# A four-row SwiGLU stream: the middle stores move from the Activation queue to the SP queue, ahead of the next loads

## The chip, the cores and the metric

The kernel runs on one core of one Trainium2 chip; the other cores of the chip run nothing of it. The metric is the device time of one execution in microseconds. Three runs of the kernel before took 964.71, 965.05 and 966.81 us, a median of 965.05 us. Beside them one execution was profiled; it took 966.08 us, of which the trace spans 964.3 us.

## The reference

```python
def setup_inputs():
    return {"x": np.random.randn(8192, 8192).astype(np.float32)}

def reference(x):
    a, b = np.split(x, 2, axis=-1)
    silu_b = b / (1 + np.exp(-b))
    return a * silu_b
```

Each of the 8192 rows holds 4096 values of `a`, then 4096 values of `b`. The output is 8192 x 4096 in float32. So 268.44 MB are read and 134.22 MB are written, 402.66 MB in all, and each element of the output needs one Silu and one product.

## The kernel before

**Tiling.** A partition takes four consecutive rows, so a group is 128 partitions x 4 rows = 512 rows, and 8192 rows make G = 16 groups (`last` is 15). The input of a group comes as two loads of 128 x 16384 float32 (8.39 MB, 64 KB in each partition): the *first* load brings rows 0 and 1 of each partition into one of two buffers, `packs[g % 2]`, and the *second* brings rows 2 and 3 into the single buffer `extra`. The output of a group, again 128 x 16384, is one store. So there are 48 transfers of equal size: 16 first loads, 16 extra loads, 16 stores.

**Compute of a group** (the function `swiglu`, lines 63 and 65). ScalarE applies Silu to `b` in place, and VectorE multiplies by `a`. It is done three times for a group: once for the two rows in the pack (128x8192), and once for each of the two rows in `extra` (128x4096). The products all go into the same pack: those of the first two rows to its first half, where the rows just read lay, and those of `extra` to its second half. The last product of a group is called `prod` in the code.

**Buffers.** `extra` is free for the next group once `prod` is there. A pack is free once its store has landed; then the first load of the group two later may fill it.

**What sets the order.** The schedule is written by hand: the kernel turns off the tile framework's own waits, and the helper `ordered` (line 42) keeps for each instruction only the waits on those handed to it and the order on its own engine. Instructions of one engine run in the order in which they are written, and a DMA is issued by an engine's sequencer: it stands at a wait until that is over, and what is written behind it on that engine stands too. A transfer of 128 partitions is spread over 16 DMA engines, in packets of 64 KB, one for each partition, so 8 on each engine: the 4896 packets of the SP queue are 34 transfers of 144, of which 128 are data and 16 mark the end, one for each DMA engine.

**The queues.** The loads are all issued by SP (the queue that the profile calls q1, line 55 in the helper `load`). Of the stores, those of groups 0 to 13 are issued by ScalarE (ACT, the queue q10, line 71 in the helper `store`) and those of groups 14 and 15 by SP. In the loop, after `prod` of group g, SP issues the extra load of group g+1; ACT at the same point issues the store of group g; and SP then waits until this store has landed, to issue the first load of group g+2.

Below, F(g) is the first load of group g, E(g) its extra load, and S(g) its store.

Of the kernel before, what the change touches and what calls it, by code (L numbers as in the profile page):

```python
# [1 line left out]

# [4 lines left out]

_SILU = mybir.ActivationFunctionType.Silu


@with_exitstack
def kernel(
    ctx: ExitStack,
    tc: tile.TileContext,
    x: bass.AP,
    out: bass.AP,
):

    nc = tc.nc
    N, M = x.shape
    half = M // 2
    P = nc.NUM_PARTITIONS
    R = 4
    W = R * half

    xv = x.tensor.reshape([N // R, R * M]).ap()
    ov = out.tensor.reshape([N // R, W]).ap()
    G = N // (P * R)
    last = G - 1

    pool = ctx.enter_context(tc.tile_pool(name="sbuf", bufs=1))
    ctx.enter_context(tc.manual_schedule())
    packs = [pool.tile([P, W], x.dtype, name=f"pack{s}") for s in range(2)]
    extra = pool.tile([P, W], x.dtype, name="extra")

    ops = []

    def ordered(inst, *after):

        before = [t for t in reversed(ops) if t.ins.engine == inst.ins.engine][:1]
        for t in ops:
            if not any(t is k for k in [*after, *before]):
                tc.declare_no_dep(inst.ins, t.ins, reason="ordered by the other waits")
        ops.append(inst)
        return inst  # L50

    def load(eng, g, h, *after):
        tile_ = extra if h else packs[g % 2]
        return ordered(
            eng.dma_start(out=tile_, in_=xv[g * P : (g + 1) * P, h * W : (h + 1) * W]), *after  # L55
        )

    def swiglu(g, h, k0, k1, *after, behind=()):

        rows = (extra if h else packs[g % 2]).rearrange("p (k s c) -> p k s c", k=2, s=2)  # L60
        o = packs[g % 2].rearrange("p (h k c) -> p h k c", h=2, k=2)
        b = rows[:, k0:k1, 1, :]
        gate = ordered(nc.scalar.activation(out=b, in_=b, func=_SILU), *after)  # L63
        return ordered(
            nc.vector.tensor_mul(out=o[:, h, k0:k1, :], in0=rows[:, k0:k1, 0, :], in1=b),  # L65
            gate, *behind,
        )

    def store(eng, g, c0, c1, *after):
        return ordered(  # L70
            eng.dma_start(out=ov[g * P : (g + 1) * P, c0:c1], in_=packs[g % 2][:, c0:c1]), *after
        )

    first = {0: load(nc.sync, 0, 0)}
    second = {0: load(nc.sync, 0, 1)}
    first[1] = load(nc.sync, 1, 0)
    for g in range(G):
        prod = swiglu(g, 0, 0, 2, first[g])
        prod = swiglu(g, 1, 0, 1, second[g], behind=[prod])
        prod = swiglu(g, 1, 1, 2, behind=[prod])  # L80
        if g < last:
            second[g + 1] = load(nc.sync, g + 1, 1, prod)
        stored = store(nc.sync if g >= last - 1 else nc.scalar, g, 0, W, prod)
        if g + 2 < G:
            first[g + 2] = load(nc.sync, g + 2, 0, stored)


# [1 line left out]
_INS = ['x']  # L89
_OUTS = [((8192, 4096), 'float32')]  # L90


# [23 lines left out]
```

## Time and profile before

| What | Value |
|---|---|
| median of three runs | 965.05 us |
| the profiled execution | 966.08 us, span 964.3 us |
| DVE busy / ACT busy | 279.2 us (29%) / 227.7 us (24%) |
| DMA packets of q1 (SP) / q10 (ACT) | 71.0% / 28.1% of the 16 engines' span |
| moved | 402.67 MB, mean 418 GB/s |
| one Silu of 128x8192 / of 128x4096 | 7.03 us / 3.61 us |
| one product of 128x8192 / of 128x4096 | 8.69 us / 4.42 us |

"q1" and "q10" are rows of the part on DMA queues: the number of packets, their bytes, and the sum of the times that these packets took as a share of 16 engines times the span. The same part can be had for any window of time; then it counts the packets that start in the window, and their whole duration, so that a share can be over 100%. From it comes the mean duration of one packet: share x window x 16 / number of packets, where packets that only mark an end (4 bytes, counted under 512 B, 9 ns) are taken out of the number.

### The profile page before, as it was taken

What the parts mean: (1) busy time and instruction counts of PE and PEld (TensorE: products, weight loads), DVE (VectorE), ACT (ScalarE), POOL (GpSimd) and SP (SyncE); (2) the same over time, 40 slices, a digit from 0 to 9 for tenths busy, and PEclk for the clock granted to TensorE, in tenths of its full rate; (3) what the DMA queues carried; (4) which work ended last, traced back from release to release, by engine and by line L of the source; (5) the groups of instructions that cost most, each with busy time, mean ns of one, the idle gap of its engine ahead of it and who ended that gap; (6) DMA issues with size and microseconds to landing.
All of it is one profiled execution on the core that took longest, in us unless ns stands there. A gap on an engine that the chain in (4) does not pass through costs nothing.

```text
span 964.3 us, 220 instructions
## 1 busy us (share of the span) xinstructions
DVE 279.2 (29%) x48; ACT 227.7 (24%) x49; POOL 0.2 (0%) x4
## 2 busy tenths in 40 slices
DVE  0423332133321333213332033321333213332250
ACT  1420222202222022220222112222022220222220
POOL 0000000000000000000000000000000000000000
DMA  9999999999999999999999999999999999999998
GB/s 400 427 435 435 413 430 421 421 432 397 435 427 402 435 394 435 424 402 435 413 435 413 391 435 400 435 427 391 435 410 430 410 405 435 392 435 416 432 410 351
DMA packets 6914, 402.67 MB, mean 418 GB/s; under 512 B 768, under 2 KB 768, under 8 KB 768
## 3 DMA queue, kind: packets, MB, share of 16 engines
q1 hardware_dynamic: 4896, 285.21, 71.0%
q10 hardware_dynamic: 2016, 117.44, 28.1%
q14 instruction: 2, 0.02, 0.0%
HBM read 268.44 MB, written 134.22 MB: 418 GB/s over the span
## 4 chain that ended last, share of the span: by engine, by line
DMA 76%; DVE 14%; ACT 6%; DVEq 0%; issue 0%; SPq 0%
DMA extra<-in_x_dram 76%; DVE pack L65 14%; ACT extra L63 6%; DVEq L111 0%; SPq L55 0%
## 5 line engine op out<-in xcount | busy, mean ns | idle before, releaser
L65 DVE TENSOR_TENSOR pack<-pack 128x8192 f32<-128x8192 f32 x16 | 139.1, 8692 | 340.8 <-ACT pack L63 340.8
L65 DVE TENSOR_TENSOR pack<-extra 128x4096 f32<-128x4096 f32 x32 | 140.2, 4421 | 317.2 <-ACT extra L63 317.2
L63 ACT ACTIVATE extra<-extra 128x4096 f32<-128x4096 f32 x32 | 114.0, 3608 | 398.4 <-DMA extra<-in_x_dram 398.4
L63 ACT ACTIVATE pack<-pack 128x8192 f32<-128x8192 f32 x16 | 112.5, 7029 | 305.1 <-DMA pack<-in_x_dram 305.1
L63 ACT ACT_TABLE_LOAD x1 | 1.3, 1283 | 0.7 <-PEq L100 0.7
L100 POOL MEMSET const-bfloat16-1.0<- 128x1 bf16 x1 | 0.1, 101 | 0.0
L100 POOL MEMSET const-uint8-127<- 128x1 uint8 x1 | 0.1, 101 | 0.0
L100 POOL MEMSET const-float32-0.0<- 128x1 f32 x1 | 0.1, 98 | 0.2 <-issue 0.2
L100 POOL MEMSET const-float32-1.0<- 128x1 f32 x1 | 0.1, 98 | 0.0
## 6 DMA issues: line engine op xcount, KB each, us to landing
pack<-in_x_dram SPq DMA_DIRECT2D x16, 29.7
extra<-in_x_dram SPq DMA_DIRECT2D x16, 47.2
out_dram<-pack ACTq DMA_DIRECT2D x14, 44.2
out_dram<-pack SPq DMA_DIRECT2D x2, 37.6
```

The source lines that it names most:

```text
L63: gate = ordered(nc.scalar.activation(out=b, in_=b, func=_SILU), *after)
L65: nc.vector.tensor_mul(out=o[:, h, k0:k1, :], in0=rows[:, k0:k1, 0, :], in1=b),
L100: nc = _bacc.Bacc("TRN2", target_bir_lowering=False, num_devices=1)
```

## The change

The loop issues all DMAs of the groups from SP, in one order. For groups 0 to 13 it is the store of group g first, then the extra load of group g+1, then, after the wait for the store, the first load of group g+2. For group 14, the order is as it was: its extra load E(15) ahead of its store. Groups 14 and 15 already stored through SP. Nothing else is touched: the same 48 transfers, tiles, and compute.

```diff
         prod = swiglu(g, 1, 1, 2, behind=[prod])
-        if g < last:
+        if g + 1 == last:
+            second[last] = load(nc.sync, last, 1, prod)
+        stored = store(nc.sync, g, 0, W, prod)
+        if g + 1 < last:
             second[g + 1] = load(nc.sync, g + 1, 1, prod)
-        stored = store(nc.sync if g >= last - 1 else nc.scalar, g, 0, W, prod)
-        if g + 2 < G:
             first[g + 2] = load(nc.sync, g + 2, 0, stored)
```

On SP, at the beginning of the program, the kernel before has these instructions (`out_dram` is the output, `in_x_dram` the input, `pack_60` and `pack_61` the two packs; the rows are F(0), E(0), F(1), E(1), F(2), E(2), F(3)):

```order
L55 DMA pack_60<-in_x_dram 128x16384
L55 DMA extra<-in_x_dram 128x16384
L55 DMA pack_61<-in_x_dram 128x16384
L55 DMA extra<-in_x_dram 128x16384
L55 DMA pack_60<-in_x_dram 128x16384
L55 DMA extra<-in_x_dram 128x16384
L55 DMA pack_61<-in_x_dram 128x16384
```

The changed kernel has, at the same place on SP, F(0), E(0), F(1), S(0), E(1), F(2), S(1), E(2), F(3):

```order
L55 DMA pack_60<-in_x_dram 128x16384
L55 DMA extra<-in_x_dram 128x16384
L55 DMA pack_61<-in_x_dram 128x16384
L71 DMA out_dram<-pack_60 128x16384
L55 DMA extra<-in_x_dram 128x16384
L55 DMA pack_60<-in_x_dram 128x16384
L71 DMA out_dram<-pack_61 128x16384
L55 DMA extra<-in_x_dram 128x16384
L55 DMA pack_61<-in_x_dram 128x16384
```

A store now stands between each first load and the extra load that follows it, in a row that was loads alone. The stores come from ACT, where the difference between the two programs reads, at the start:

```order
-L63 ACTIVATE pack_60<-pack_60 128x2x4096
-L63 ACTIVATE extra<-extra 128x4096 x2
-L71 DMA out_dram<-pack_60 128x16384
-L63 ACTIVATE pack_61<-pack_61 128x2x4096
-L63 ACTIVATE extra<-extra 128x4096 x2
-L71 DMA out_dram<-pack_61 128x16384
```

The Silus stand in the changed program in the same order; the 14 stores between them are gone from ACT.

## The prediction

> **What bounds the kernel now.** I read the page first: busy times, then the DMA queues.
>
> ```profile
> span 964.3 us, 220 instructions
> DVE 279.2 (29%) x48; ACT 227.7 (24%) x49; POOL 0.2 (0%) x4
> ...
> q1 hardware_dynamic: 4896, 285.21, 71.0%
> q10 hardware_dynamic: 2016, 117.44, 28.1%
> ...
> pack<-in_x_dram SPq DMA_DIRECT2D x16, 29.7
> extra<-in_x_dram SPq DMA_DIRECT2D x16, 47.2
> out_dram<-pack ACTq DMA_DIRECT2D x14, 44.2
> out_dram<-pack SPq DMA_DIRECT2D x2, 37.6
> ```
>
> The compute engines are busy for under a third; the packets of the two queues fill 71.0 + 28.1 = 99.1% of the DMA engines' time. So the kernel is a stream of packets, and it can become shorter only if packets take less time or if the 0.9% between them shrinks. The question is then whether 99.1% is all useful, that is, what one packet takes when nothing disturbs it. For that I took the DMA queues in windows of four kinds: loads alone (24 to 40 us), loads and stores mixed (300 to 335 us), stores alone (942 to 958 us):
>
> ```profile
> DMA packets 112, 7.34 MB, mean 459 GB/s; under 512 B 0, under 2 KB 0, under 8 KB 0
> q1 hardware_dynamic: 112, 7.34, 105.8%
> ...
> DMA packets 252, 15.27 MB, mean 436 GB/s; under 512 B 19, under 2 KB 19, under 8 KB 19
> q10 hardware_dynamic: 121, 7.73, 51.0%
> q1 hardware_dynamic: 131, 7.54, 49.7%
> ...
> DMA packets 113, 7.14 MB, mean 446 GB/s; under 512 B 4, under 2 KB 4, under 8 KB 4
> q1 hardware_dynamic: 113, 7.14, 103.0%
> ```
>
> A load packet: 1.058 x 16 us x 16 / 112 = 2.42 us. Mixed: 7.73 MB are 118 packets of 65536 B, 0.510 x 35 x 16 / 118 = 2.42 us for a store; 7.54 MB are 115 packets, 0.497 x 35 x 16 / 115 = 2.42 us for a load. Stores alone: 1.030 x 16 x 16 / 109 = 2.42 us. A packet costs the same in either direction, alone or mixed. A transfer is 128 packets, 8 on each engine: 8 x 2.42 = 19.3 us. All 48 need 928.5 us (with 2.418). The span is 35.8 us longer. Where these go is seen from the period, in the chain of waits:
>
> ```profile
> 42.07 3.62 ACT extra L63
> ...
> 353.33 47.35 DMA extra<-in_x_dram
> 400.69 0.02 issue
> 400.71 3.62 ACT extra L63
> 404.33 0.02 issue
> 404.36 8.77 DVE pack L65 x2
> 413.13 0.02 issue
> 413.14 47.69 DMA extra<-in_x_dram
> ...
> 882.34 3.62 ACT extra L63
> ```
>
> From the landing of E(0) to that of E(14) are 14 groups in 882.34 - 42.07 = 840.3 us, 60.02 us for a group. Three transfers need 24 x 2.418 = 58.03 us, so **1.99 us of each group are lost**, 27.9 us in 14; the other 8 us are start and end, which the change leaves alone. A period of 60 us has two places of loss, both seen in windows. The first is where a store joins the loads, 354.85 to 356.9 us, just behind the issue at 353.33; the second where F comes, issued only when the store has landed, with E almost through (398.5 to 402.5 us). The rows of the timeline give the start, the length and the issue; then come the windows in the same order:
>
> ```profile
> 353.33 0.36 ACTq L71 DMA_DIRECT2D out_dram<-pack  x1
> 397.25 0.33 SPq L55 DMA_DIRECT2D pack<-in_x_dram  x1
> ...
> DMA packets 16, 1.05 MB, mean 512 GB/s; under 512 B 0, under 2 KB 0, under 8 KB 0
> q1 hardware_dynamic: 16, 1.05, 183.0%
> ...
> DMA packets 31, 1.44 MB, mean 360 GB/s; under 512 B 9, under 2 KB 9, under 8 KB 9
> q1 hardware_dynamic: 31, 1.44, 103.2%
> ```
>
> First place: 16 load packets, one on each engine, take 1.83 x 2.05 = 3.75 us instead of 2.42, a loss of **1.33 us**. Second place: 22 data packets take 1.032 x 4 x 16 / 22 = 3.00 us each, and some engines find their queue empty for a moment. Its whole price is what remains: 1.99 - 1.33 = **0.66 us**.
>
> **The change, part by part.** It makes one row of packets on each engine: ... F(g+1), S(g), E(g+1), F(g+2), S(g+1) ...
>
> *The empty queue before F goes: -0.66 us a group.* Now S(g) lands a whole E ahead of the point at which F(g+2) is needed. SP issues F on that landing, with about 19.3 us of E(g+1) still ahead of it, and needs some 2 us (a landing and an issue; below). Some 17 us are to spare, so F's packets stand ready when E's end.
>
> *Store joining loads: 1.33 becomes 0.63 us.* The kernel before has one place where a store follows a load on one queue: E(15), then S(14), both on SP. The timeline has the issue of S(14) at 895.16 us (its row joins both stores of SP), and the window from 917.9 to 920.3 us holds the last load packet of most engines before S(14):
>
> ```profile
> 895.16 42.45 SPq L71 DMA_DIRECT2D out_dram<-pack  x2
> ...
> DMA packets 16, 1.05 MB, mean 437 GB/s; under 512 B 0, under 2 KB 0, under 8 KB 0
> q1 hardware_dynamic: 16, 1.05, 127.1%
> ```
>
> 1.271 x 2.4 = 3.05 us, a loss of 0.63 us. I take that for each of the 14 turns F(g+1) to S(g); its bounds are 0 (the mixed window, where every change of direction on an engine is free) and 1.33 (the store on its own queue). The row of the same queue is the nearest.
>
> *New: the turn from store to load on one queue, S(g) to E(g+1), 14 times.* Before has none. From below it is 0: in the mixed window each engine goes from a q10 store to a q1 load every other packet, at 2.42 us. From above I take 1.33, the dearest turn in the trace. Between them lies a load that starts with nothing of its kind under way, the first of the program, 1.7 to 3.7 us:
>
> ```profile
> 0.73 0.38 SPq L55 DMA_DIRECT2D pack<-in_x_dram  x1
> ...
> q1 hardware_dynamic: 16, 1.05, 152.8%
> ```
>
> 1.528 x 2.0 = 3.06 us, a loss of 0.64 us. A gain from the turn itself has no row: in none of the undisturbed windows does a packet take under 2.42 us. I take 0.64, because the opposite turn on one queue, with all its packets waiting in the row, also cost 0.63: that packets stand ready did not make that turn free, as two queues do.
>
> The Trainium skill, "DMA: Bandwidth & Descriptors", section "Two DMAs through the same engine are not ordered", says that in one queue descriptors start in order but are pipelined, and that an engine's read and write sides are separate queues. By that, a load's reading would begin under the store's writing and the turn would cost nothing; the turn of 0.63 us that the trace shows in the other direction does not agree that overlap is complete.
>
> *Is S(g) there in time?* It is queued when `prod` is there, 413.14 - 400.71 = 12.4 us behind the landing of E(g). The cover is F(g+1), 19.3 us on each engine. From the first issue (0.73 us) to its first packets passes about 1 us, and I allow as much from the last packet to the landing: 19.3 - 12.4 - 2 = about 5 us are left. Were they gone, each us of lateness would cost 14 us in all.
>
> *Issues.* SP takes over 14 issues of 0.36 us and the wait for `prod`, which E(g+1) had there anyway. Behind the wait for S(g)'s landing stand F(g+2) and then S(g+1), whose `prod` comes a whole load later. All lies under the transfers: 0. ACT loses the issues, and only waits longer for data: 0.
>
> *Sum.* Lost per group: 0.63 + 0.64 = 1.27 us, instead of 1.99. The gain is 0.72 us x 14 = 10.1 us. Span: 964.3 - 10.1 = 954.2; the profiled execution's own time, 966.08, would be 956.0. The runs' median stands 1.03 us below that time, so the forecast is 965.05 - 10.1 = **955.0 us**.
>
> **The rivals.**
>
> *The turn to loads is free.* For it: mixed packets turn for nothing. Against it: the 0.63 above. The skill's sentence on read and write sides, above, is this rival. The loss is then 0.63 a group, the gain 1.36 x 14 = 19.0, and the time 946.0 us.
>
> *It only trades losses.* If the turn to loads costs 1.33, a group loses 0.63 + 1.33 = 1.96 us: gain 0.4 us, 964.6 us. For it: a load waits for data from afar and a store has it at hand, so this turn could be the dearer of the two. Against it: even the cold start of a load cost 0.64 only. The Trainium skill, same page, "Issuing engines are not separate DMA queues", has it that DMAs of all issuing engines end on the same 16 engines and that issuing from several saves sequencer time alone. By that the queue's name would change nothing and the time would stay at 965.05; the trace shows 1.33 against 0.63 us for the same turn, so it doesn't quite bear it out.
>
> *Slower: two separate queues were what kept the engines full.* In the mixed stretch of before, an engine has a packet of either direction at hand; with one row it drains at each turn. If both turns cost 1.33, a group loses 2.66 us, 0.67 more than now: 9.4 us more, 974.4 us. It decides where the two turns together pass 1.99 us. For it: the only price known for the turn into stores in mid-stream is 1.33, and the 0.63 is one place at the end, with the store queued 23 us ahead of its turn; in the loop it is queued about 5 us ahead. Against it: three of four prices of a fresh start lie near 0.6.
>
> *The change does not do what it says:* F still comes late, or S(g) does. The spare 17 and 5 us speak against both.
>
> **How the numbers follow.** A difference under 0.2%, or 1.9 us, can't be told from none here; the three runs themselves span 0.2%. Chances: the forecast (the turn to loads between 0.3 and 1.0 us) 0.40; the free turn 0.28; traded losses 0.16, of which I give a fourth to a gain over 1.9 us; slower by draining queues 0.12; something not seen, 0.04, halved between the sides. Faster: 0.40 + 0.28 + 0.04 + 0.02 = 0.74; the same: 0.12; slower: 0.12 + 0.02 = 0.14. The range reaches from the free turn with its turn into stores a little cheaper than measured, 944, to just past the trade, 966. It leaves out the slower case and little else.
>
> **What would show it.** The profile after should have one busy queue q1 of 6912 packets. If the order works, a store lands about 27 us after its issue (5 of F, 19.3 of its own, turns and landing) instead of 44.2, an extra load still after about 47, and a first load after about 38 instead of 29.7. The period should be 58.03 + 1.27 = 59.3 us; 58.7 says that the turn to loads is free, 60 that it costs 1.33. The windows about the turns show it packet by packet: about 3.05 us for the last load before a store, and about as much for the packet on the turn from store to load. The prediction is wrong if the packets in mid-transfer are no longer 2.42 us, if engines stand without a packet between F(g+1) and S(g), or if a turn costs over 1.36 us.

## The result, and the profile after

The changed kernel takes 939.2 us (median of four runs, 938.51 to 940.43) against 965.22 us before (four runs by now): a ratio of 0.9729, 95% interval 0.9712 to 0.9746. It is 26 us faster, where 10 were forecast, and it lies below the range of 944 to 966 us. The page of the profiled execution (938.51 us):

```profile
span 936.4 us, 220 instructions
...
q1 hardware_dynamic: 6912, 402.66, 99.5%
...
pack<-in_x_dram SPq DMA_DIRECT2D x16, 38.8
extra<-in_x_dram SPq DMA_DIRECT2D x16, 45.3
out_dram<-pack SPq DMA_DIRECT2D x16, 26.4
```

One queue with all 6912 packets, busy 99.5% of the span. The order works as it was worked out: a store lands 26.4 us after its issue (27 foretold), an extra load after 45.3 (47), a first load after 38.8 (38). The period, from the chain of waits, first and last of the 14 groups, and one store's issue between (start, length, what):

```profile
42.10 3.63 ACT extra L63
...
230.12 0.34 SPq L71
...
858.24 3.62 ACT extra L63
```

(858.24 - 42.10) / 14 = 58.30 us, against 60.02 before and 58.03 for three undisturbed transfers. So a group loses 0.27 us on average, no longer 1.99. That is 1.72 x 14 = 24.1 us of the span's 27.9; the other 3.8 come from what lies behind E(14), 964.3 - 882.34 = 82.0 us before and 936.4 - 858.24 = 78.2 us now. The turns, in windows of the DMA queues: first 57.5 to 60 us, the last load packets before S(0); then 640 to 760 us, two whole periods in the later part of the run:

```profile
q1 hardware_dynamic: 16, 1.05, 132.2%
...
DMA packets 907, 52.23 MB, mean 435 GB/s; under 512 B 110, under 2 KB 110, under 8 KB 110
q1 hardware_dynamic: 907, 52.23, 100.6%
```

The first turn from loads to a store costs 1.322 x 2.5 = 3.31 us for a packet of 2.42, 0.89 us on every engine. The two periods hold 797 data packets at 1.006 x 120 x 16 / 797 = 2.42 us, through two turns to stores and two to loads. So this late in the run both turns of the one queue cost next to nothing, but the first turn did. Why, is what the runs below were for.

### The profile page after: what moved, and what is told of

It reads as the page before. It is cut to its first block, busy times and chain, and to the rows that moved or that the text cites. A ratio compares the mean times of both kernels' runs of the same rounds, so it can differ in the third digit from the quotient of the medians.

```text
span 936.4 us, 220 instructions
## 1 busy us (share of the span) xinstructions
DVE 279.2 (30%) x48; ACT 227.7 (24%) x49; POOL 0.2 (0%) x4
## 3 DMA queue, kind: packets, MB, share of 16 engines
q1 hardware_dynamic: 6912, 402.66, 99.5%
## 4 chain that ended last, share of the span: by engine, by line
DMA 75%; DVE 15%; ACT 6%; SPq 1%; DVEq 0%; issue 0%
DMA extra<-in_x_dram 75%; DVE pack L65 15%; ACT extra L63 6%; SPq L71 1%; DVEq L112 0%; SPq L55 0%
## 6 DMA issues: line engine op xcount, KB each, us to landing
pack<-in_x_dram SPq DMA_DIRECT2D x16, 38.8
extra<-in_x_dram SPq DMA_DIRECT2D x16, 45.3
out_dram<-pack SPq DMA_DIRECT2D x16, 26.4
```

## The experiments

Two theories stood against each other after the result. By the first, 1.33 us was the price of a transfer on a queue of its own that had run empty, and the change removed it by leaving that queue. By the second it had to do with the loads, and the queue's name had nothing to do with it. The kernel before, run again beside two of the groups of experiments, had medians of 966.15 and 967.25 us, and beside the third a single run of 962.33 us, so that times of different groups can be compared to a few us only. The run with the late store and the runs of transfers alone were made once each.

**Old order, one queue.** Only the issuing engine of the stores is changed in the kernel before:

```diff
-        stored = store(nc.sync if g >= last - 1 else nc.scalar, g, 0, W, prod)
+        stored = store(nc.sync, g, 0, W, prod)
```

> The kernel before with one thing changed: every store is issued by SP too, but in the old order, extra load E(g+1), then store S(g), then first load F(g+2). The forecast's view (a queue that runs empty costs): S(g) is now the last thing in the row, F(g+2) is issued only on its landing, so each engine stands for a landing and an issue, about 2.2 us, and starts cold, 0.6 us: a period of about 60.8 us against 58.3 of the changed kernel, 972 to 978 us in all. Rival (one queue is what helps, the order is not): no loss where the store joins and little at F, period about 58.5 to 59.3, 940 to 953 us.

Measured: 987.13 us, a ratio to the kernel before of 1.0209 (1.0172 to 1.0246), slower still than expected. Windows of 385.6 to 386.3 us (the last load packets before a store) and 410.3 to 410.7 us (the first packets of the late F):

```profile
q1 hardware_dynamic: 16, 1.05, 501.9%
...
q1 hardware_dynamic: 16, 1.05, 796.7%
```

The turn takes 5.019 x 0.7 = 3.51 us, a loss of 1.09 in mid-run, with all on one queue and the store long in the row. The late F starts at 7.967 x 0.4 = 3.19 us, 0.77 too much, and the timeline has the issues of F at

```profile
347.93 0.33 SPq L55 DMA_DIRECT2D pack<-in_x_dram  x1
409.42 0.33 SPq L55 DMA_DIRECT2D pack<-in_x_dram  x1
```

61.49 us apart: 58.03, 0.77 and 1.09 leave 1.6 us in which the engines stood idle. One queue by itself is no help at all. The first theory is in trouble: the store has no queue of its own here and costs nearly what it cost before.

**The extra load on ACT's queue**, store and first load on SP, in the new order:

```diff
-            second[g + 1] = load(nc.sync, g + 1, 1, prod)
+            second[g + 1] = load(nc.scalar, g + 1, 1, prod)
```

(E(15) has a line of its own and stayed on SP, other than the expectation says.)

> The changed kernel with its extra loads E(1) to E(14) issued by ACT instead of SP (E(15), too); stores and first loads stay on SP. If a transfer that arrives on a queue which had run empty costs every engine about 1.3 us, whatever its direction, E pays it now, and F(g+2), which finds nothing ahead of it, another 2.8: a period of about 62 us, 985 to 997 us. If only a store that arrives pays, E joins for nothing: period about 60.8, 970 to 978 us. If two queues cost nothing in themselves: under 965 us.

Measured: 987.5 us, ratio 1.0213 (1.0181 to 1.0244). The number is the one that the first theory had named, but the trace does not bear out the reason. E is issued on ACT at 288.02 us, and from 300 to 320 us it runs beside F; 324.2 to 325.1 us holds E's packets ahead of the first store packet, which now comes on the queue of the loads:

```profile
q1 hardware_dynamic: 79, 5.18, 59.7%
q10 hardware_dynamic: 64, 4.19, 48.4%
...
q10 hardware_dynamic: 16, 1.05, 385.0%
```

Beside F, E's packets take 0.484 x 20 x 16 / 64 = 2.42 us. The stretched packets stand at the turn to the store, 3.85 x 0.9 = 3.47 us, a loss of 1.05. What costs is the turn, and its price does not go with the queue.

**The store some us after the extra load**, on its own queue, in the kernel before:

```diff
+            for _ in range(3):
+                reads.append(ordered(nc.scalar.activation(out=idle, in_=packs[g % 2][:, W - 1024 :], func=_SILU), prod))
         stored = store(nc.sync if g >= last - 1 else nc.scalar, g, 0, W, prod)
```

> The kernel before with three short Silus on ACT (128x1024, into a tile that nobody uses) between the last product and the store of groups 0 to 13, so the store is issued some 3 us after the extra load instead of in the same instant. If the loss of 1.33 us comes from two sequencers that issue at once, the packets at the join take 2.42 to 2.6 us now. If it comes from the store's queue having run empty, they still take about 3.7 us, some 3 us later than before. The time goes up in either case, to 975 to 1005 us, since the store ends later and F(g+2) with it.

(`idle` is a tile that nobody reads, and the first load that follows waits for these Silus too.) Measured: 1003.72 us in the one run. The two issues, and the window of 238.7 to 240 us:

```profile
234.73 0.33 SPq L56 DMA_DIRECT2D extra<-in_x_dram  x1
236.92 0.34 ACTq L72 DMA_DIRECT2D out_dram<-pack  x1
...
q1 hardware_dynamic: 16, 1.05, 280.2%
```

The issues are 2.2 us apart, and the packets at the join take 2.802 x 1.3 = 3.64 us as ever. Two sequencers that issue in the same instant are not the cause.

**Three groups put back, on two queues.** In the changed kernel, groups 4, 8 and 12 as they were before:

```diff
-        if g + 1 == last:
+        if g + 1 == last or g in (4, 8, 12):
             second[g + 1] = load(nc.sync, g + 1, 1, prod)
-        stored = store(nc.sync, g, 0, W, prod)
+        stored = store(nc.scalar if g in (4, 8, 12) else nc.sync, g, 0, W, prod)
```

(and the extra load behind the store is left out for these groups)

> The changed kernel with groups 4, 8 and 12 as in the kernel before (extra load first on SP, store on ACT). Each of the three should bring back its 1.7 to 2.0 us: 939.2 + 5 to 6 = 944 to 945 us, if the losses are a group's own. What the next turn from loads to a store on SP (groups 5, 9, 13) costs tells two theories of the 0.88 us apart that the first turn of the changed kernel cost, against 0 to 0.13 of the later ones: if a queue's first store pays, they pay nothing; if engines pay that turn in step, and a late F sets them in step again, they pay 0.6 to 0.9 us again, and the time is 946 to 947 us.

Measured: 956.61 us (954.44 to 957.93), ratio 0.9889 (0.9856 to 0.9922): 17.4 us more than the changed kernel, far over what either theory had. The window of 350.3 to 351.4 us, the turn to S(5), which is on SP again:

```profile
q1 hardware_dynamic: 16, 1.05, 316.0%
```

3.16 x 1.1 = 3.48 us: 1.06 us lost at a turn on one queue that had had four stores before, and that in the changed kernel costs about 0.1 us at this place. What came ahead of it is F(6), late because S(4) went by ACT. So a queue's first store is not the cause. Most of the 17 us lies in one stretch of mixed packets and the wait behind it, to which I come back at the end.

**Transfers alone.** To get rid of compute and of the late F together, a stream without Silu and product: a load that is held, then 32 loads into two tiles in turn, and 16 stores of the held tile. First with all on SP, then with the stores on ACT, each issued when a load has landed:

```diff
-        store(nc.sync, g, 0, W, held)
+        landed(2 * g)
+        store(nc.scalar, g, 0, W, held)
```

(`landed` is a Silu of 128x8 that reads the tile of that load, so that ACT waits for it; it stands at the beginning of the loop.)

> Transfers alone, no Silu and no product (the output is the first tile in all places): one load into a pack, then 32 loads of the same shape into two tiles in turn, and 16 stores out of that pack, one behind every second load, all on SP with always two transfers in the row. 49 transfers need 49 x 19.34 = 947.9 us, and about 6 at the start and end. If a turn on one queue is free after the first: span 953 to 956 us. If each turn costs 0.6: 963 to 973 us.

> The same transfers, with the 16 stores issued by ACT, each when one load has landed and the next is running, so that the store's queue has run empty before each and the loads' queue never does. If a store that arrives on an empty queue costs 1.33 us: span 973 to 977 us, and packets of about 3.7 us at each join. If the loss of before came from the late first load alone: 953 to 957 us.

Measured: spans of 956.4 and 965.7 us. Windows of 100 to 940 us of the first, of 43.3 to 44.1 us (the first join), 102.2 to 103.1 us (the second join) and 60 to 940 us of the second:

```profile
DMA packets 6263, 364.32 MB, mean 434 GB/s; under 512 B 704, under 2 KB 704, under 8 KB 704
q1 hardware_dynamic: 6263, 364.32, 100.3%
...
q1 hardware_dynamic: 16, 1.05, 411.3%
...
q1 hardware_dynamic: 16, 1.05, 272.4%
...
q1 hardware_dynamic: 4348, 253.04, 67.2%
q10 hardware_dynamic: 2157, 125.63, 33.0%
```

On SP, 5559 data packets take 1.003 x 840 x 16 / 5559 = 2.42 us through some 14 turns each way. On two queues the first join costs 4.113 x 0.8 = 3.29 us, 0.87 lost. The second takes 2.724 x 0.9 = 2.45 us a packet and costs almost nothing. From 60 us on 3861 load packets take 0.672 x 880 x 16 / 3861 = 2.45 us: 0.03 us more than undisturbed, about 8 us an engine over some 15 joins, half a microsecond each on average. A store's queue that runs empty before each store is thus not worth 1.33 us; most of that goes away when the loads never run dry. The two missed spans say the same: 956.4 is just past the upper end of the free turn, and 965.7 lies between the two theories, in part for a reason of its own (below).

**Does a long time without a store matter?** One queue, with the stores behind loads 4, 10, 16 and 28:

```diff
+        if k in (3, 9, 15, 27):
+            store(nc.sync, done, 0, W, held)
```

> The same transfers on SP alone, with the stores behind the loads number 4, 10, 16 and 28 and the other 12 at the end, so that the second to fourth store come after 116, 116 and 232 us of loads. If only the queue's first store costs its 0.6 to 0.9 us, the packets ahead of the later ones take 2.42 us. If the cost depends on how long no store ran, each of them takes about 3.0 to 3.3 us.

Measured: span 953.0 us. Windows of 96.5 to 97.1 us (the first turn) and 200 to 500 us (two more):

```profile
q1 hardware_dynamic: 16, 1.05, 547.9%
...
DMA packets 2224, 130.02 MB, mean 433 GB/s; under 512 B 240, under 2 KB 240, under 8 KB 240
q1 hardware_dynamic: 2224, 130.02, 100.1%
```

The first turn: 5.479 x 0.6 = 3.29 us. Then 1984 data packets at 1.001 x 300 x 16 / 1984 = 2.42 us: nothing, after 116 us of loads. It isn't time without a store.

**Loads that join loads.** Every third load issued by ACT, the stores all at the end:

```diff
+        if k % 3 == 2:
+            landed(k - 2)
+        next_load(nc.scalar if k % 3 == 2 else nc.sync)
```

> The same transfers, with every third load issued by ACT when another has landed, and all 16 stores at the end on SP. So 10 times a load arrives on a queue that has run empty while loads run on the other; there is no change of direction. If an empty queue that gets work costs 1.33 us whatever the direction: span 966 to 969 us and packets of about 3.7 us at the joins. If only stores pay: 953 to 956 us and 2.42 us.

Measured: span 969.9 us, a little above the higher of the two figures. But the joins themselves are free, as in the window of 50 to 60 us, and the turn to the first store (653 to 657 us) costs most of all:

```profile
q1 hardware_dynamic: 32, 2.10, 48.4%
q10 hardware_dynamic: 32, 2.10, 48.4%
...
q1 hardware_dynamic: 16, 1.05, 97.1%
```

0.484 x 10 x 16 / 32 = 2.42 us on either queue at the join; 0.971 x 4 = 3.88 us at the turn. So again the time could have been read as the price of a queue, and the packets say otherwise: the loss lies at the ten loads that SP issues late in this order, where the trace shows 0.15 to 1.9 us without a packet (mean of the 16 engines) and slow first packets.

**The new theory, and its test.** Each dear turn above has a start behind it, of all 16 engines at once: the program's start, or a late load. Then either each engine owes something for its first turn after a start, or the 16 engines, which a common start has set in step, get in each other's way when they turn to stores together. First the late F on one queue, three times in the changed kernel, with the edit of the run on two queues but all on SP:

```diff
-        if g + 1 == last:
+        if g + 1 == last or g in (4, 8, 12):
             second[g + 1] = load(nc.sync, g + 1, 1, prod)
         stored = store(nc.sync, g, 0, W, prod)
```

> The changed kernel with groups 4, 8 and 12 in the order of the kernel before, extra load, then store, then first load, but all of it on SP. New theory (a late first load is the one cause: the queue runs empty, the engines start again together, and their next turn from loads to a store costs over 1 us whatever the queue): each of the three costs 1.9 idle + 0.7 cold + 1.1 at the next turn = 3.7 us, 939.2 + 11 = 950 us, with packets of 3.4 to 3.8 us ahead of the stores of groups 5, 9 and 13. Rival (it is ACT's queue that costs): no loss beyond the 2.6 us of each late load, 947 us, and 2.42 to 2.6 us packets ahead of those stores.

Measured: 952.32 us (951.65 to 954.71), ratio 0.9834 (0.975 to 0.9917), 13.1 us more than the changed kernel, 4.4 for each late F (3.7 expected). The window of 354.2 to 354.8 us, the turn to S(5):

```profile
q1 hardware_dynamic: 16, 1.05, 605.0%
```

6.05 x 0.6 = 3.63 us, 1.21 lost, where the changed kernel lost about 0.1 us. ACT's queue has no part in it.

Then the start from empty in the middle of the bare stream: two loads more, each of which waits until the store before it has landed, so that the queue runs empty.

```diff
+        if g in (5, 10):
+            held = ordered(nc.sync.dma_start(out=packs[0], in_=xv[0:P, 0:W]), stored)
```

> The transfers alone on SP, in the order of the run on one queue, with two loads more, behind the stores of groups 5 and 10, that wait until that store has landed, so the one queue runs empty twice in the middle. If a start from empty brings the turn's cost back, the packets ahead of the next store take 3.3 to 3.5 us again, two transfers or more behind the start, and those of the other later stores 2.4 to 2.7. If only the first store of a queue pays, none of the later ones does. Span 51 x 19.34 = 986.5 us, 6 to 7 at the ends and about 3.7 for each empty queue: 999 to 1002 us; 997 by the rival.

Measured: span 1002.9 us. Windows of 449 to 452 us (the first turn behind the first restart, three loads later), 508.5 to 510 us (the next turn) and 763 to 766 us (the first behind the second restart):

```profile
q1 hardware_dynamic: 16, 1.05, 110.4%
...
q1 hardware_dynamic: 16, 1.05, 173.3%
...
q1 hardware_dynamic: 16, 1.05, 114.9%
```

1.104 x 3 = 3.31 us, 1.733 x 1.5 = 2.60 us, 1.149 x 3 = 3.45 us. The restart brings the price back, at the first turn above all. The next pays 0.18; the dearest later turn pays 0.51 (880.9 to 881.9 us, 16 packets at 2.93 x 1 = 2.93 us).

Last, what decides between the two forms of the theory: the bare stream on SP, with two small loads in front that give some engines more to do.

```diff
+    ordered(nc.sync.dma_start(out=spare[0:88], in_=xv[0:88, 0:3584]))
+    ordered(nc.sync.dma_start(out=spare[96:121], in_=xv[96:121, 0:3584]))
```

> The transfers alone on SP, as in the run with all on one queue, with two small loads in front (88 and 25 partitions of 14 KB into a tile that nobody uses) that give some of the 16 engines several packets more than others, so that the engines reach the first turn from loads to a store some us apart. If the cost of 0.9 to 1.1 us comes from all engines turning at once, the packets ahead of the first store take clearly less now, 2.4 to 2.9 us. If each engine pays for its own first turn after a start, they take 3.3 to 3.5 us as before, only at two or three different times.

Measured: span 964.6 us, 8 more than without them: engines that begin late end late. The packets show three sets: 5 engines start the first big load at 4.2 to 4.7 us, 6 at 9.6 to 10.3, 5 at 15.4 to 15.6, and they reach the first store in the same sets, 2.5 to 3 us apart, between 85 and 94 us. The window of 70 to 100 us:

```profile
DMA packets 224, 12.91 MB, mean 430 GB/s; under 512 B 27, under 2 KB 27, under 8 KB 27
q1 hardware_dynamic: 224, 12.91, 99.4%
```

197 data packets at 0.994 x 30 x 16 / 197 = 2.42 us. The first turn costs nothing any more, on any engine. With the same stream in step it cost 1.0 us (76 to 79 us of the run on one queue, 16 packets at 1.142 x 3 = 3.43 us; the run with restarts, made beside this one, has 3.30 us there):

```profile
q1 hardware_dynamic: 16, 1.05, 114.2%
```

So no engine owes anything by itself: the first turn is dear when all 16 make it together. But turning together is not enough, and the theory is too simple there. In the changed kernel the engines are as close together at the second turn as at the first: windows of 57.8 to 58.7 us and of 116.8 to 117.6 us each hold all 16 packets ahead of the store, S(0) and S(1).

```profile
q1 hardware_dynamic: 16, 1.05, 367.3%
...
q1 hardware_dynamic: 16, 1.05, 318.9%
```

3.673 x 0.9 = 3.31 us the first time, 3.189 x 0.8 = 2.55 us the second: 0.89 and 0.13 us lost. So the price wears off before the engines have drifted apart. What makes it wear off, and what the engines share at the dear turn, the runs do not show.

Nor need the engines stand still at the late load. In the kernel before, F(2) is issued at 98.30 us, when the last packets of E(1) have just begun (at 97.6 to 98.2 us). Its own first packets (99.9 to 100.7 us, with 16 end marks) follow without a gap, and yet the turn behind it (116.8 to 117.6 us) is dear:

```profile
98.30 0.33 SPq L55 DMA_DIRECT2D pack<-in_x_dram  x1
...
q1 hardware_dynamic: 32, 1.05, 306.6%
...
q1 hardware_dynamic: 13, 0.85, 349.0%
```

F(2) starts at 3.066 x 0.8 = 2.45 us a packet, undisturbed; at the turn 13 engines take 3.49 x 0.8 x 16 / 13 = 3.44 us (the other three turn a packet earlier). What the dear turns shown here have in common is that the queue of the loads had no packet left to start when the next load was issued. Idle engines and slow first packets can come on top.

## Why the prediction was right or wrong

*That the stream of packets is the bound, and 2.42 us a packet in every mix:* right for these two kernels (two of the runs had slower mixes, below). The changed kernel's span comes within 8 us of the 928.5 us of 48 transfers.

*The empty queue before F goes:* right in its place, and too small in what hangs on it. I priced it at 0.66 us, the rest that was left of 1.99 after the join of the store.

*Store joining loads, 1.33 becomes 0.63:* this is the step that failed. I took 1.33 us for a price of the store's own queue, and the 0.63 of the place behind E(15) for the price on one queue. By the runs both are the same thing, a turn behind a late F, since F(15) before that place is late as well (issued at 879.71 us, with E(14) almost through). With F on time the turn costs 0.89 us once and then at most 0.2. So the late F stands behind both losses: idle engines and slow first packets where it comes, and a dear turn one transfer later. On one queue this is shown, since a late F that is put back brings the dear turn back. For the two queues of the kernel before it is inferred, from the transfers alone with stores on ACT, where the loads never ran dry and the second join cost 0.03 us. The size was off as well: read packet by packet, the 14 turns of the kernel before lost 0.5 to 1.6 us, 1.2 in the mean, and 1.33 is the one that I had looked at. The row I called the nearest was nearest by the queue's name, and had the same late load ahead of it.

*The turn from store to load, 0.64:* wrong by its whole size; it costs nothing (640 to 760 us above). The Trainium skill, "DMA: Bandwidth & Descriptors", section "Two DMAs through the same engine are not ordered", says that the descriptors of one queue are pipelined and that an engine's read and write sides are separate queues. By that this turn is free, and the trace agrees, with 2.42 us a packet. I had set the rule aside because of the 0.63 us in the other direction, which was no property of a queue.

*Start and end, which the change leaves alone:* wrong by 3.8 us. The end before held the late F(15) and the dear turn to S(14), and both are gone; what each was worth was not measured.

The 24.1 us of the groups and the 3.8 behind them are the span's 27.9 us cut at one point, and prove nothing by themselves. The two pages say of what kind the gain is: packets filled 0.991 x 964.3 = 955.6 us of an engine's time before and 0.995 x 936.4 = 931.7 now. So 23.9 us come from packets that are no longer stretched, and 4.0 from engines that no longer stand without one.

*The rivals.* The free turn (946 us) had the right mechanism for one of the two turns. Traded losses and draining queues are refuted, each with a turn to loads that costs nothing. The Trainium skill, same page, section "Issuing engines are not separate DMA queues", has it that the DMAs of all issuing engines end on the same 16 engines, so that the queue's name should change nothing. In the old order it did (965.22 against 987.13 us), but through the order in which the transfers end. On two queues E and S share the engines and the store ends shortly before E; on one, S behind E ends last of all and F waits longer (987.13 us), and S ahead of E ends a transfer early (939.2 us).

## What to carry to other kernels

Where a stream of DMAs is the bound, look for the transfer that is issued when nothing of its queue is left, and put whatever it waits for a whole transfer ahead of that point; a late transfer costs its idle time, slow first packets, and another loss at the next turn from loads to a store. Price a loss by what came before it, not by the place where its packets are stretched: a stretched packet at the join of two queues looked like a price of the second queue, and was the echo of a load that came late a transfer earlier. When a run's total agrees with a theory, read the packets too; twice here the number came out as one theory had it, or nearly, with the loss in another place.

## What the runs showed of the hardware that was not expected

- Behind a load that found its queue with nothing left to start, sixteen engines lost 0.5 to 1.6 us each at the next turn from loads to a store; in three sets, 2.5 to 3 us apart, they lost nothing. Later turns cost 0 to 0.5 us, even where the engines were no further apart. No other distance was tried on purpose.
- Mixed loads and stores on two queues are not always free. They were in the window of 300 to 335 us of the kernel before (436 GB/s), but in two of the runs some such stretches ran slower. First the run with the late store, 300 to 335 us, then the run with three groups put back on ACT, 770 to 800 us:

```profile
DMA packets 209, 12.65 MB, mean 361 GB/s; under 512 B 16, under 2 KB 16, under 8 KB 16
q1 hardware_dynamic: 116, 6.55, 53.7%
q10 hardware_dynamic: 93, 6.09, 43.3%
...
DMA packets 166, 10.81 MB, mean 360 GB/s; under 512 B 1, under 2 KB 1, under 8 KB 1
q1 hardware_dynamic: 79, 5.11, 50.1%
q10 hardware_dynamic: 87, 5.70, 46.6%
```

A load packet takes 0.537 x 35 x 16 / 100 = 3.01 us there and 0.501 x 30 x 16 / 78 = 3.08 us, a store packet 2.61 and 2.57 us. In the second of these runs E(12), E(13) and E(14) landed at 747.73, 813.30 and 875.86 us, 12 us more than two undisturbed periods; the two other groups put back cost 2.1 and 3.4 us by the same reckoning. So the third of them alone makes most of the 17 us. Why these stretches and not others stays open.
- Two queues can let the engines drift apart. The bare stream with stores on ACT still moved 1.77 MB in the last 12 us of its span (953 to 965 us), on some engines only; on one queue the last 4.6 us (951.4 to 956) held 0.13 MB:

```profile
DMA packets 42, 1.77 MB, mean 147 GB/s; under 512 B 15, under 2 KB 15, under 8 KB 15
...
DMA packets 12, 0.13 MB, mean 29 GB/s; under 512 B 10, under 2 KB 10, under 8 KB 10
```

The spans differ by 9.3 us for the same transfers. The pages of the run on one queue and of the run on two tell the parts:

```profile
q1 hardware_dynamic: 7056, 411.04, 99.5%
...
q1 hardware_dynamic: 4752, 276.83, 67.0%
q10 hardware_dynamic: 2304, 134.22, 32.1%
```

Packets fill 0.995 x 956.4 = 951.6 us of an engine's time on one queue and 0.991 x 965.7 = 957.0 on two. So some 5 us are slower packets, and the other 4 are engines that stand without one, mostly at this uneven end.
